# Hi and lo parts of the weights written from the second element of tiles one element longer

## The chip, the cores and the metric

The kernel runs on one NeuronCore of one Trainium2 chip. The metric is the device time of one execution, in microseconds. The engines named below are PE (TensorE, the matrix engine), PEld (its weight loads, which the profile lists by themselves), DVE (VectorE), ACT (ScalarE), POOL (GpSimd) and SP (SyncE, which only issues transfers here). Of the kernel before, three runs are known and one profiled execution.

## The reference

One step of a hybrid decoder layer in 32-bit floats, for 512 prompt tokens and 8 sample tokens, 520 columns together, with a model width of 2048:

```
xn   = rmsnorm(x) ; proj = xn @ w_in            # 2048 x 6160
ya   = bg * causal_conv3(cg * hin)              # short convolution, 1024 channels
yb   = rmsnorm(gla(q, k, v, gate)) * silu(og)   # gated linear attention, 4 heads
x    = x + concat(ya, yb) @ w_out               # 2048 x 2048
u, v = split(rmsnorm(x) @ w_up)                 # 2048 x 11264
x    = x + (silu(causal_conv3(u) + b) * v) @ w_down   # 5632 x 2048
y    = rmsnorm(x)
```

The outputs are y for both kinds of tokens and the new states of the convolutions and of the attention. Nearly all of the arithmetic is in the four products with `w_in`, `w_out`, `w_up` and `w_down`.

## The kernel before

Activations lie transposed: 128 channels on the partitions, 520 token columns along them, cut into two halves of 260 columns (`HT`). A matmul holds a 128 x 128 block of weights still and streams 260 columns past it.

Each operand is kept as two parts. The hi part is the value as the format `float32r` holds it (the ACT copy rounds it), the lo part is what is left. A product is then three matmuls, hi with hi, hi with lo and lo with hi (`mm3`, and the same three in `up_product` and `chunk_product`). For the weights this goes piece by piece: a piece of 128 x 1024 weights is loaded into a tile `raw`, ACT writes its hi part into a tile `hi`, DVE subtracts and writes the lo part into a tile `lo`, and PE reads eight 128 x 128 blocks from each. The pool `wp` keeps three tiles each of `raw`, `hi` and `lo`, of 1024 elements a partition.

There are two ways in which pieces are made:

- `parts` (lines 107 to 116) in the first stage, the plain products (`group`, with the matmuls on line 140), and again at the very end. ACT writes `hi` on line 111 and DVE writes `lo` on line 112.
- `prepare` (lines 1179 to 1200) in the long middle of the program. There the two-by-two blocks of a matrix product are multiplied in seven products instead of eight, some of them with sums of weight blocks (`raw`, or the sum tile `s`) as the source. ACT writes `hi` on line 1194, DVE writes `lo` on line 1198. Products are numbered by `order`; the loop calls `prepare(i + 2)` right after it has issued the matmuls of product `i`, so a piece is made about two products ahead of its use. `up_product` (matmuls on line 1218) and `chunk_product` (line 1461) use one hi and one lo tile for 24 matmuls.

The order of the work on PE, DVE and ACT, and in stretches on POOL and SP, is the program's own: `InOrder` ties each instruction to the one before it on its engine. Weights come over SP's queue; POOL's queue carries the stores of the activations' parts and some sums made by transfers that add. After the first stage follow a mixing stage with nine groups of seven products, eight groups for `w_out`, 44 for `w_up` and 20 for `w_down`, and then the end with plain products and the last norm.

For the steps of the prediction these places matter too: `conv_rest` (line 530) reads a padded tile from its second element (`i` is 1) and then from its first; `level` (lines 894 and 897) multiplies every other run of elements, and at the last of its seven levels, where a run is one element, line 894 reads and writes every second element beginning with the second, and line 897 every second beginning with the first. The matmul on line 943 holds 32 columns still instead of 128. At the end, one half of the tokens has 264 columns and the other 256.

Of the kernel before, what the change touches and what calls it, by code (L numbers as in the profile page):

```python
# [10 lines left out]
F32R = mybir.dt.float32r  # L11
# [6 lines left out]
P = 128  # L18
# [19 lines left out]
def trunk_kernel(  # L38
# [12 lines left out]
    wp = ctx.enter_context(tc.tile_pool(name="weights", bufs=3))  # L51
# [47 lines left out]
    def load(w, k0, nk, c0, ncol):  # L99
# [4 lines left out]
        )  # L104
        return raw, nk

    def parts(raw, nk):
        n = raw.shape[1]
        hi = wp.tile([P, 1024], F32R, tag="hi", name="hi")[:, :n]
        lo = wp.tile([P, 1024], F32R, tag="lo", name="lo")[:, :n]  # L110
        nc.scalar.activation(hi, raw, AF.Copy)  # L111
        nc.vector.tensor_tensor(lo, raw, hi.bitcast(F32), op=ALU.subtract)  # L112
        return (
            hi.rearrange("p (k c) -> p k c", k=nk),
            lo.rearrange("p (k c) -> p k c", k=nk),
        )

    def piece(*where):
        return parts(*load(*where))
# [157 lines left out]
    with ExitStack() as es:  # L277
# [164 lines left out]
        x_split(0)  # L442
        warm(8)
        ws = [parts(raws[0], 8)]
        x_copy(1)
        x_split(1)
# [4 lines left out]
        for k in range(KD):  # L451
# [11 lines left out]
            if t == 1 and c < 3:  # L463
                ws.append(parts(raws[c + 1], 8))
# [701 lines left out]
    state, his, los = {}, {}, {}  # L1166
# [12 lines left out]
    def prepare(i):  # L1179


        def sum_next():
            if i + 1 < len(order):
                kind, at, r = order[i + 1]
                if r in state[kind, at]["sums"]:
                    state[kind, at]["sums"][r]()

        if i >= len(order):
            return
        in_place = i + 1 < len(order) and order[i + 1][2] == 6  # L1190
        kind, at, r = order[i]
        src = state[kind, at]["src"][r]
        his[i] = wp.tile([P, 1024], F32R, tag="hi", name="hi")
        nc.scalar.activation(his[i], src, AF.Copy)  # L1194
        if not in_place:
            sum_next()
        los[i] = wp.tile([P, 1024], F32R, tag="lo", name="lo")
        nc.vector.tensor_tensor(los[i], src, his[i].bitcast(F32), op=ALU.subtract)  # L1198
        if in_place:
            sum_next()  # L1200
# [433 lines left out]
    ps = new_mm()  # L1634
    span(ps, ws[0], xa, 0, 0, 8, KD)
    prepare(0)
    for x in put[:3]:
        x()
    span(ps, ws[1], xa, 8, 8, 8, KD)
    prepare(1)  # L1640
    for x in put[3:6]:
        x()
# [25 lines left out]
    for i, (kind, at, r) in enumerate(order):  # L1668
        j, n = i % 7, i // 7
# [41 lines left out]
        if i in (0, 2, NW, NW + 2):  # L1711

            x = xq[1, 0][0]
            for ps in new[:2] if i in (0, NW) else new[2:]:
                nc.tensor.matmul(ps[:, :HT], x[:, :P], x, start=True, stop=True)
        prepare(i + 2)
        if j == 5 and more:
            state[groups[n + 1]]["seventh"]()
# [187 lines left out]
```

## Time and profile before

| | |
|---|---|
| runs | 2180.01, 2180.38, 2180.81 us |
| median of the runs | 2180.38 us |
| profiled execution, its span | 2180.4 us |
| instructions | 43803 |
| PE, busy | 2152.9 us, 99% |
| PEld, busy | 2131.3 us, 98% |
| DVE, busy | 1735.7 us, 80% |
| ACT, busy | 1114.0 us, 51% |
| POOL, busy | 438.1 us, 20% |

The profile is of one execution. Its span and the median of the runs are the same number to the tenth of a microsecond. A matmul's own duration in the records is longer than the distance from its start to the next one's start, since matmuls overlap in the pipeline; so the rate of PE is read from starts, or from the number of matmuls in a stretch. "hi" and "lo" in a row are the weights' parts; yh, yl, b, bh, bl, xh, xl, ch, cl and form are tiles of activations, which stream past.

### The profile page before, as it was taken

Reading aid. Unit: us, or ns where it says so; the run is one execution under the profiler, and the core shown is the slowest. Engines: PE = TensorE matmul, PEld = TensorE weight load, DVE = VectorE, ACT = ScalarE, POOL = GpSimd, SP = SyncE. Lnnn points to the kernel's source line nnn. Section 1 sums busy time; section 2 is a strip of 40 time slices with the busy share of each in tenths; the row PEclk is TensorE's granted clock in tenths of the full one; section 3 lists DMA queues with packets and bytes.
Section 4 is the critical chain, followed back from the end, with each engine's and each line's share of the span. In section 5 each row is a group of like instructions: output and inputs, shape, how many; then the busy total and the mean of one; then the engine's idle time right before and its main releaser. Section 6 shows DMA issues by size and latency. Waiting matters only on the chain.

```text
span 2180.4 us, 43803 instructions
## 1 busy us (share of the span) xinstructions
PE 2152.9 (99%) x17751; PEld 2131.3 (98%) x17751; DVE 1735.7 (80%) x2298; ACT 1114.0 (51%) x1625; POOL 438.1 (20%) x625
## 2 busy tenths in 40 slices
PE   9999999999999999999999999999999999999997
PEld 8999999999999999999999999999999999999997
DVE  6346465578888897988888988998998778888886
ACT  6335435355544586555555555555555553444445
POOL 4213131121243321121221131122111310010000
PEclk9999999999999999999999999999999999999999
DMA  8545464387788996667676676676677886894734
GB/s 247 147 125 158 122 191 124 92 246 210 204 257 248 297 266 176 179 178 187 164 189 174 165 195 176 163 194 177 171 186 190 285 202 197 248 271 132 226 107 156
DMA packets 467163, 415.51 MB, mean 191 GB/s; under 512 B 21641, under 2 KB 426393, under 8 KB 466817
## 3 DMA queue, kind: packets, MB, share of 16 engines
q1 hardware_dynamic: 424081, 289.71, 46.5%
q0 software_dynamic: 42832, 122.93, 21.4%
q8 instruction: 139, 2.28, 0.4%
q14 instruction: 63, 0.52, 0.1%
q10 hardware_dynamic: 48, 0.07, 0.0%
HBM read 299.45 MB, written 80.31 MB: 174 GB/s over the span
## 4 chain that ended last, share of the span: by engine, by line
PE 88%; DMA 4%; DVE 3%; issue 1%; ACT 1%; POOL 1%; SPq 0%; ACTq 0%; DVEq 0%; POOLq 0%
PE mm L1218 34%; PE mm L140 16%; PE ms L1218 14%; PE y L1461 7%; PE x L1461 7%; PE f L1461 3%; PE e L1461 3%; PE ms L957 1%; DMA raw<-in_w_out_dram 1%; DMA form<-g_d 1%; DVE lo L1198 1%; DMA g_d<-fh 1%; DMA x_d<-acc 1%; DMA yl<-t_d 0%; DMA raw<-in_w_down_dram 0%
## 5 line engine op out<-in xcount | busy, mean ns | idle before, releaser
L1218 PE MATMUL mm<-yl,hi 128*128 128x260 f32 x1696 | 479.8, 283 | 3.6 <-DVE yl L124 3.6
L1218 PE MATMUL mm<-yh,hi 128*128 128x260 f32 x1696 | 480.5, 283 | 2.1 <-ACT ms L1228 1.8
L1218 PE MATMUL mm<-yh,lo 128*128 128x260 f32 x1696 | 479.8, 283 | 0.8 <-DVE lo L1198 0.8
L1194 ACT ACTIVATE hi<-raw 128x1024 fp32r<-128x1024 f32 x324 | 342.6, 1057 | 233.9 <-PE mm L1218 69.0
L1198 DVE TENSOR_TENSOR lo<-raw,hi 128x1024 fp32r<-128x1024 f32 x324 | 395.2, 1220 | 41.2 <-ACT hi L1194 40.7
L1198 DVE TENSOR_TENSOR lo<-s,hi 128x1024 fp32r<-128x1024 f32 x243 | 298.3, 1228 | 127.2 <-ACT hi L1194 121.9
L1194 ACT ACTIVATE hi<-s 128x1024 fp32r<-128x1024 f32 x243 | 256.9, 1057 | 217.2 <-DVE s L1139 80.2
L1218 PEld LDWEIGHTS mm<-yl,hi 128*128 128x128 f32 x1696 | 320.1, 189 | 4.2 <-DVE yl L124 4.2
L1218 PEld LDWEIGHTS mm<-yh,hi 128*128 128x128 f32 x1696 | 319.7, 189 | 2.7 <-ACT ms L1228 2.0
L1218 PEld LDWEIGHTS mm<-yh,lo 128*128 128x128 f32 x1696 | 320.4, 189 | 1.2 <-DVE lo L1198 1.2
L1218 PE MATMUL ms<-b,hi 128*128 128x260 f32 x1408 | 257.8, 283 | 0.0
L1218 PEld LDWEIGHTS ms<-b,hi 128*128 128x128 f32 x1408 | 218.5, 190 | 0.0
L1461 PE MATMUL x<-form,hi 128*128 128x260 f32 x1120 | 204.6, 283 | 0.8 <-DVE acc L1480 0.8
L1461 PE MATMUL y<-form,hi 128*128 128x260 f32 x1120 | 204.5, 282 | 0.5 <-DVE acc L1480 0.5
L1139 DVE TENSOR_TENSOR s<-s,raw 128x1024 f32<-128x1024 f32 x162 | 197.8, 1221 | 2.8
L1218 PE MATMUL ms<-b,lo 128*128 128x260 f32 x704 | 199.5, 283 | 0.0
L1461 PEld LDWEIGHTS x<-form,hi 128*128 128x128 f32 x1120 | 172.4, 188 | 1.2 <-issue 1.0
L1461 PEld LDWEIGHTS y<-form,hi 128*128 128x128 f32 x1120 | 172.5, 188 | 0.8 <-issue 0.7
L1461 PE MATMUL y<-form,lo 128*128 128x260 f32 x560 | 158.2, 283 | 0.8 <-DVE lo L1198 0.8
L1461 PE MATMUL x<-form,lo 128*128 128x260 f32 x560 | 158.1, 282 | 0.0
L112 DVE TENSOR_TENSOR lo<-raw,hi 128x1024 fp32r<-128x1024 f32 x76 | 93.7, 1238 | 78.2 <-ACT hi L111 71.6
L1218 PEld LDWEIGHTS ms<-b,lo 128*128 128x128 f32 x704 | 133.4, 190 | 0.0
(366 smaller groups left out, 5077.8 us busy)
## 6 DMA issues: line engine op xcount, KB each, us to landing
raw<-in_w_up_dram SPq DMA_DIRECT2D x176, 512.0 KB, 4.7
raw<-in_w_down_dram SPq DMA_DIRECT2D x96, 512.0 KB, 5.5
raw<-in_w_in_dram SPq DMA_DIRECT2D x92, 512.0 KB, 4.4
form<-f_d SPq DMA_DIRECT2D x126, 260.0 KB, 6.8
raw<-raw POOLq DMA_DIRECT2D x56, 512.0 KB, 5.5
f_d<-t POOLq DMA_DIRECT2D x80, 260.0 KB, 5.5
raw<-in_w_out_dram SPq DMA_DIRECT2D x32, 512.0 KB, 12.7
form<-g_d POOLq DMA_DIRECT2D x42, 260.0 KB, 7.7
```

The lines of the kernel that those rows point to most:

```text
L112: nc.vector.tensor_tensor(lo, raw, hi.bitcast(F32), op=ALU.subtract)
L140: nc.tensor.matmul(o, w, xx, start=first and i == 0, stop=last and i == 2)
L957: nc.tensor.matmul(pb[:, c * 64 : (c + 1) * 64], L[:, c, :], rhs[:, c], start=True, stop=True,)
L1139: return lambda: nc.vector.tensor_tensor(out, x, y, op=ALU.add)
L1194: nc.scalar.activation(his[i], src, AF.Copy)
L1198: nc.vector.tensor_tensor(los[i], src, his[i].bitcast(F32), op=ALU.subtract)
L1218: nc.tensor.matmul(st["bank"][b], w[:, k, :], x, start=b not in st["used"] and k == 0 and j == 0, stop=k == 7 and j == 2, skip_group_check ...
L1461: nc.tensor.matmul(ps[:, m, :], w[:, k, m * P : (m + 1) * P], x, start=b not in st["used"] and k == 0 and j == 0, stop=k == 3 and j == 2, ...
```

## The change

The tiles of the weights' parts get 1025 elements a partition instead of 1024, and what is written and read is the slice from the second element on. Both places where such tiles are made now call the same small function; nothing else is changed. The elements written and read, the instructions, their order and their waits are the same as before. The first element of each tile is neither written nor read. The data of each part so begins 4 bytes behind the start of its tile, and the six tiles take a little more of each partition.

```diff
+    def offset(tag):
+
+        return wp.tile([P, 1025], F32R, tag=tag, name=tag)[:, 1:]
+
     def parts(raw, nk):
         n = raw.shape[1]
-        hi = wp.tile([P, 1024], F32R, tag="hi", name="hi")[:, :n]
-        lo = wp.tile([P, 1024], F32R, tag="lo", name="lo")[:, :n]
+        hi, lo = (offset(tag)[:, :n] for tag in ("hi", "lo"))
         nc.scalar.activation(hi, raw, AF.Copy)
         nc.vector.tensor_tensor(lo, raw, hi.bitcast(F32), op=ALU.subtract)
...
-        his[i] = wp.tile([P, 1024], F32R, tag="hi", name="hi")
+        his[i] = offset("hi")
         nc.scalar.activation(his[i], src, AF.Copy)
         if not in_place:
             sum_next()
-        los[i] = wp.tile([P, 1024], F32R, tag="lo", name="lo")
+        los[i] = offset("lo")
         nc.vector.tensor_tensor(los[i], src, his[i].bitcast(F32), op=ALU.subtract)
```

## The prediction

> **What bounds the kernel now.** I read the page's busy shares first, then its chain of work that ended last, then the table of windows.
>
> ```profile
> PE 2152.9 (99%) x17751; PEld 2131.3 (98%) x17751; DVE 1735.7 (80%) x2298; ACT 1114.0 (51%) x1625; POOL 438.1 (20%) x625
> ...
> PEclk9999999999999999999999999999999999999999
> ...
> PE 88%; DMA 4%; DVE 3%; issue 1%; ACT 1%; POOL 1%; SPq 0%; ACTq 0%; DVEq 0%; POOLq 0%
> ```
>
> PE is busy for 99% of the span at the full granted clock, and 88% of the chain is PE's. The span, 2180.4 us, and the median of the runs, 2180.38 us, agree, so I add and subtract from 2180.4 directly. The windows say how fast PE goes and what the others do meanwhile (columns: length, then busy time and instructions of PE, PEld, DVE, ACT and POOL, clock, DMA share, GB/s):
>
> ```profile
> 412.00:600.00 188.00, 185.20 (x1519) 184.17 (x1518) 149.25 (x204) 95.67 (x140) 37.35 (x53) 0.99 0.75 202
> 600.00:780.00 180.00, 179.50 (x1494) 179.09 (x1494) 154.13 (x176) 96.84 (x132) 68.26 (x94) 1.00 0.91 262
> ...
> 1200.00:1400.00 200.00, 200.00 (x1672) 200.00 (x1672) 177.91 (x239) 108.32 (x161) 41.55 (x60) 1.00 0.69 179
> ...
> 1900.00:2100.00 200.00, 200.00 (x1673) 200.00 (x1672) 167.76 (x170) 84.17 (x90) 9.20 (x12) 1.00 0.62 186
> ```
>
> In 1200 to 1400 us, 1672 matmuls start in 200 us, one each 119.6 ns. From 1900 to 2100 us DVE, ACT, POOL and the transfers do less, other tiles stream past, and the number is 1673. So the step of 119.6 ns does not depend on how busy the others are. It is PE's own, and the kernel's time is roughly that step times the matmuls. One nanosecond on each of the matmuls that use hi and lo is worth 17 us: they are 567 pieces of the middle part (324 and 243 in the rows of line 1198 below) times 24, 13,608, and those of the 76 pieces of line 112; 17,751 is the number of all matmuls. I use 17,000.
>
> **The change, part by part.** No instruction, byte of transfer or wait is added or removed. What moves is an address: three kinds of access now begin at an odd 4-byte word. These are ACT's writes of hi, DVE's reads of hi and writes of lo, and PE's loads from both.
>
> ```profile
> L1194 ACT ACTIVATE hi<-raw 128x1024 fp32r<-128x1024 f32 x324 | 342.6, 1057 | 233.9 <-PE mm L1218 69.0
> L1198 DVE TENSOR_TENSOR lo<-raw,hi 128x1024 fp32r<-128x1024 f32 x324 | 395.2, 1220 | 41.2 <-ACT hi L1194 40.7
> L1198 DVE TENSOR_TENSOR lo<-s,hi 128x1024 fp32r<-128x1024 f32 x243 | 298.3, 1228 | 127.2 <-ACT hi L1194 121.9
> ...
> L112 DVE TENSOR_TENSOR lo<-raw,hi 128x1024 fp32r<-128x1024 f32 x76 | 93.7, 1238 | 78.2 <-ACT hi L111 71.6
> ```
>
> DVE first. The trace has contiguous reads from an odd word: line 530 reads its padded tile from the second element, and two rows later from the first. It also has writes to odd words, though one element at a time: the last level on line 894, beside line 897 on even ones.
>
> ```profile
> 210.88 0.41 DVE L894 TENSOR_TENSOR L<-e,q 128x256 f32<-128x256 f32 x1
> 211.22 0.41 DVE L897 TENSOR_TENSOR L<-e,k 128x256 f32<-128x256 f32 x1
> ...
> 1006.91 0.74 DVE L530 SCALAR_TENSOR_TENSOR t<-zpad,parf,t 128x512 f32<-128x512 f32 x1
> 1007.58 0.22 DVE L533 SCALAR_TENSOR_TENSOR t<-stf,parf,t 128x8 f32<-128x8 f32 x1
> 1007.71 0.74 DVE L530 SCALAR_TENSOR_TENSOR t<-zpad,parf,t 128x512 f32<-128x512 f32 x1
> ```
>
> 0.74 against 0.74 us and 0.41 against 0.41 us: odd reads and odd writes cost nothing that shows. The lower end for a lo is therefore 0; for the upper end I take the dearest instruction of this kind beside a plain one of its length, both scalar_tensor_tensor with two tensors:
>
> ```profile
> L612 DVE SCALAR_TENSOR_TENSOR t<-t 128x260 f32<-128x260 f32 x56 | 23.8, 425 | 0.9
> ...
> L930 DVE SCALAR_TENSOR_TENSOR s<-s,asm,vb 128x256 f32<-128x256 f32 x32 | 20.5, 676 | 15.2 <-issue 5.2 <-ACT vb L927 4.8 <-DMA s<-in_state_gla_dram 3.8
> ```
>
> 676 / 425 = 1.6, or 0.73 us more on 1.22 us. I take 0, the value of the nearest rows. The cover is DVE's idle time: in 1200 to 1400 us it is 200 - 177.9 = 22.1 us, and about 70 pieces are made there (1672 / 24), so up to 22.1 / 70 = 0.32 us a piece costs nothing but slack.
>
> [...]
>
> ACT's write of hi has no odd row beside it. It is bounded by 0 and, by the same 1.6, 0.63 us on 1.06 us; ACT is busy 108.3 of 200 us there, so even 70 x 0.63 = 44 us fits. A piece is made two products ahead, 2 x 24 x 119.6 ns = 5.7 us before PE wants it, and hi and lo together could grow by 1.36 us inside that. If this cover failed, the next to be late would be PE, in the wait for lo that its rows show at 0.8 us or so now.
>
> PE's weight loads remain, and these nothing covers but PE's own step.
>
> ```profile
> L1218 PEld LDWEIGHTS mm<-yh,lo x1696: 186/188/334, 463.7 to 1707.2; 128*128 128x128 f32 x189
> ...
> L1461 PE MATMUL x<-form,lo x560: 277/282/296, 647.2 to 2098.1; 128*128 128x260 f32 x187
> L1461 PEld LDWEIGHTS y<-form,lo x560: 186/188/193, 650.2 to 2112.4; 128*128 128x128 f32 x187
> ```
>
> ```profile
> L943 PEld LDWEIGHTS ms<-s,qm x64: 106/108/110, 113.1 to 393.8; 128*32 128x32 f32 x64
> ```
>
> A load of 128 columns takes 188 ns, one of 32 columns 108 ns (min/median/max): (188 - 108) / 96 = 0.83 ns a column, so 107 ns of the 188 are the columns and the rest overlaps. 107 ns fit into a step of 119.6 ns with 13 ns to spare. That the streamed columns and not the load set the step is seen at the end of the program, where 264 and then 256 columns stream past the same kind of load:
>
> ```profile
> 2121.56 0.28 PE L140 MATMUL mm<-bh,lo 128*128 128x264 f32 x1
> ...
> 2122.66 0.28 PE L140 MATMUL mm<-bh,lo 128*128 128x264 f32 x1
> ```
>
> ```profile
> 2152.30 0.28 PE L140 MATMUL mm<-bl,hi 128*128 128x256 f32 x1
> ...
> 2153.36 0.28 PE L140 MATMUL mm<-bl,hi 128*128 128x256 f32 x1
> ```
>
> Nine steps lie between the two rows each time: 1.10 us / 9 = 122 ns and 1.06 / 9 = 118 ns. If an odd start adds one access to a load, a column's 0.83 ns or a few of them, it vanishes in the 13 ns.
>
> What the trace can't say is whether the load and the stream disturb each other. The durations of undisturbed matmuls spread from 277 over 282 to 296 ns in the row of line 1461 above, although columns and clock are the same. So something of PE's own varies by -5 to +14 ns, and I take these as the two ends for the unknown effect of the odd start on the step: -5 x 17,000 = -85 us and +14 x 17,000 = +238 us. I take 0, since no row ties the spread to the weights' first word. The sum is 2180.4 + 0 = 2180.4 us.
>
> **The rivals.**
> *Loads and streams collide less (faster).* For it: the step is 119.6 ns though the load needs 107, the matmuls vary among themselves, and the other engines' load does not explain it. Against it: nothing shows the start word as the cause. At half of the lower end, -2.5 ns, the time is 2180.4 - 42 = 2138 us; at the whole, 2095 us.
> *The load pays for the odd start (slower).* The place is the load of every 128 x 128 block, and it decides once the columns of a load need more than 119.6 instead of 107 ns, 12% more, or once they disturb the stream. At a quarter of the upper end, +3.5 ns, the time is 2180.4 + 60 = 2240 us; at the whole 2418 us. Against it: the 13 ns to spare.
> *DVE pays for the odd start (slower).* It decides from 0.32 us a piece. At the upper end, 0.73 us, DVE needs 177.9 + 70 x 0.73 = 229 us for each 200 us of the middle part, 15% more for the 900 us from 800 to 1700 us, and 167.8 + 51 = 219 us, a tenth more, for the 400 us behind them: 135 + 40 us, near 2355 us. The rows of lines 530 and 894 speak against it. [...]
> *Only the other tiles' moved places matter.* The six tiles grow, so all that lies behind them moves. A shift of 0.3 to 0.6 ns in the step, either way, is 5 to 10 us: 2170 or 2190 us.
>
> **How the numbers follow.** No change that can be measured: 0.42, with its own range of 2176 to 2185 us. Less collision: 0.28. The load pays: 0.16. DVE pays: 0.06. Moved places: 0.08, half each way. A measurement of this kernel tells 0.2%, 4.4 us, from no change. So faster is 0.28 + 0.04 = 0.32, the same 0.42, slower 0.16 + 0.06 + 0.04 = 0.26. The likeliest is 2180.4 us. The range has to reach into both sides: down to 2105 us, which leaves out the last part of the first rival (about 0.06), and up to 2240 us, which leaves out half of the load's rival and most of DVE's (about 0.13).
>
> **What would show it.** If I am right, 200 us of the middle part still hold 1672 matmuls, loads stay at 188 ns, lo at 1.22 us, hi at 1.06 us, and PE's idle time before lo stays near 1 us. More matmuls in 200 us, with DVE unchanged, would be the first rival; fewer, with PE still without idle time, the second; lo beyond 1.5 us and PE idle behind DVE's lo the third. The forecast is wrong if the count in such a window differs by more than 3 from 1672.

## The result and the profile after

The kernel with the longer tiles takes 2186.66 us (median, 2186.07 to 2189.67) against 2180.38 us (2179.46 to 2181.16). The ratio is 1.0032, with a 95% interval of 1.0021 to 1.0043: slower by 0.3%. That lies inside the range given, but further from the likeliest case, no change at all, than the 0.2% that the prediction took for measurable.

The page of the kernel after, its span and its busy times:

```profile
span 2188.0 us, 43803 instructions
...
PE 2160.2 (99%) x17751; PEld 2138.0 (98%) x17751; DVE 1737.7 (79%) x2298; ACT 1115.2 (51%) x1625; POOL 438.7 (20%) x625
```

PE has 7.3 us more busy time (2152.9 before), DVE 2.0 and ACT 1.2 us more; the span grew by 2188.0 - 2180.4 = 7.6 us. So PE's growth is nearly the whole of it. (These are two single executions, and that of the changed kernel was the longest of its seven runs; the medians lie 6.3 us apart.) The windows of the kernel after (columns as above):

```profile
600.00:780.00 180.00, 179.11 (x1485) 178.36 (x1484) 153.07 (x178) 95.36 (x131) 69.52 (x95) 1.00 0.89 260
...
1200.00:1400.00 200.00, 200.00 (x1665) 200.00 (x1664) 178.16 (x240) 108.32 (x161) 41.52 (x60) 1.00 0.67 176
...
1900.00:2100.00 200.00, 200.00 (x1667) 200.00 (x1666) 167.81 (x169) 83.29 (x90) 9.19 (x12) 1.00 0.61 186
```

PE still has no idle time in the middle part and the clock is full, but 200 us now hold 1665 matmuls and not 1672: by the count the step is 120.12 ns where it was 119.62. (A window also counts the two or three matmuls that begin before it and reach into it. Of the 1672, 1670 start in the window; steps taken from the starts, as below, are therefore 0.2 ns longer, for every kernel alike.) Near the end there are 1667 for 1673. What feeds PE is unchanged, as the groups of the kernel after show (line numbers are 3 higher):

```profile
L1201 DVE TENSOR_TENSOR lo<-raw,hi 128x1024 fp32r<-128x1024 f32 x324 | 396.2, 1223 | 44.0 <-ACT hi L1197 43.4
L1197 ACT ACTIVATE hi<-raw 128x1024 fp32r<-128x1024 f32 x324 | 343.2, 1059 | 236.8 <-PE mm L1221 69.0 <-issue 62.7 <-PE y L1464 25.7
...
L1221 PE MATMUL mm<-yh,lo 128*128 128x260 f32 x1696 | 480.7, 283 | 0.9 <-DVE lo L1201 0.9
```

A lo takes 1223 ns for 1220, a hi 1059 for 1057, and PE's idle time before lo is 0.9 us for 0.8. The loads keep their time too:

```profile
L1464 PEld LDWEIGHTS y<-form,lo x560: 187/188/194, 653.1 to 2119.8; 128*128 128x128 f32 x187
L1464 PE MATMUL y<-form,lo x560: 277/282/388, 653.2 to 2119.9; 128*128 128x260 f32 x187
```

188 ns, and 282 ns for a matmul, are the medians of before. The loss is therefore in no single instruction; it is in the distance between them. I took the distances from each matmul's start to the next one's, for the matmuls of the plain, mix, up, `w_out` and down products, wherever a distance lay between 100 and 140 ns in both traces (16,635 of them):

| kernel | all three | plain (L140) | mix and up (L1218) | w_out and down (L1461) | matmuls in 1200-1400 us |
|---|---|---|---|---|---|
| before | 119.86 ns | 120.08 | 119.80 | 119.81 | 1672 |
| after | 120.28 ns | 120.56 | 120.29 | 120.08 | 1665 |

16,635 x 0.425 ns = 7.1 us of the 7.6 us lie in these steps, spread over the whole program. The rest, 0.5 us, lies elsewhere.

Theory A: an odd word at the start of a block costs PE's step. Theory B: the odd word is innocent, and the growth of the tiles is at fault, since it puts each weights' tile at another distance from the last and moves the tiles behind it.

### The profile page after: what moved, and what is told of

Read it like the earlier page. It is cut to its first block, busy times and chain, and to the rows that moved or that the text cites. A ratio compares the mean times of both kernels' runs of the same rounds, so it can differ in the third digit from the quotient of the medians.

```text
span 2188.0 us, 43803 instructions
## 1 busy us (share of the span) xinstructions
PE 2160.2 (99%) x17751; PEld 2138.0 (98%) x17751; DVE 1737.7 (79%) x2298; ACT 1115.2 (51%) x1625; POOL 438.7 (20%) x625
## 4 chain that ended last, share of the span: by engine, by line
PE 60%; DMA 2%; DVE 1%; issue 1%; ACT 0%; POOL 0%; ACTq 0%; DVEq 0%; SPq 0%; POOLq 0%
PE mm L1221 29%; PE ms L1221 12%; PE y L1464 6%; PE x L1464 6%; PE f L1464 3%; PE e L1464 3%; PE mm L143 2%; DMA ssq<-fh 1%; DMA x_d<-acc 1%; DMA raw<-in_w_down_dram 0%; PE ms L1804 0%; DVE lo L1201 0%; DMA yl<-t_d 0%; DVE yl L127 0%; DVE s L1142 0%
## 5 line engine op out<-in xcount | busy, mean ns | idle before, releaser
L1197 ACT ACTIVATE hi<-raw 128x1024 fp32r<-128x1024 f32 x324 | 343.2, 1059 | 236.8 <-PE mm L1221 69.0
L1201 DVE TENSOR_TENSOR lo<-raw,hi 128x1024 fp32r<-128x1024 f32 x324 | 396.2, 1223 | 44.0 <-ACT hi L1197 43.4
L1197 ACT ACTIVATE hi<-s 128x1024 fp32r<-128x1024 f32 x243 | 257.4, 1059 | 217.5 <-PE ms L1221 86.2
```

## The experiments

All times in this table are medians of their own runs, the ratio is to runs of the kernel before beside them on the same chip, and the steps are worked out as above.

| run | us | ratio, 95% interval | step, ns | matmuls in 1200-1400 us |
|---|---|---|---|---|
| e1_grow | 2180.63 | 0.9999 (0.9990 to 1.0008) | 119.91 | 1670 |
| e2_ring0 | 2179.47 | 0.9997 (0.9988 to 1.0006) | 119.87 | 1672 |
| e3_ring1 | 2185.74 | 1.0024 (1.0014 to 1.0034) | 120.29 | 1663 |
| e4_off4 | 2181.33 | 1.0000 (0.9991 to 1.0009) | 119.89 | 1670 |
| e5_hi1 | 2188.92 | 1.0032 (1.0020 to 1.0043) | 120.34 | 1663 |
| e6_lo1 | 2184.68 | 1.0011 (1.0002 to 1.0020) | 120.04 | 1669 |
| e7_off2 | 2184.00 | 1.0011 (1.0002 to 1.0020) | 120.02 | 1670 |
| e11_slices3 | 2172.06 | 0.9964 (0.9951 to 0.9976) | 119.20 | 1679 |
| e12_slices0 | 2179.75 | 1.0001 (0.9992 to 1.0010) | 119.86 | 1673 |

### Growth without the offset

```diff
-        return wp.tile([P, 1025], F32R, tag=tag, name=tag)[:, 1:]
+        return wp.tile([P, 1025], F32R, tag=tag, name=tag)[:, :1024]
```

> The tiles of hi and lo are 1025 elements wide as in the changed kernel, but their first 1024 elements are used, so nothing begins at an odd word. Theory A (the odd 4-byte word costs the step of PE): back to 1671-1673 matmuls in 1200-1400 us and 2180 us. Theory B (the places count: each tile begins 4128 instead of 4096 bytes behind the one before, and the tiles behind them move by 96 to 192 bytes): as the changed kernel, about 1665 matmuls there and 2185-2188 us, and not the same in each of its places.

The windows of this run:

```profile
1200.00:1400.00 200.00, 200.00 (x1670) 200.00 (x1670) 177.90 (x238) 108.13 (x161) 41.06 (x60) 1.00 0.67 178
```

1670 matmuls and 2180.63 us: the growth and everything that it moves cost nothing that the times can tell. Theory B, as put, falls.

### The offset without the growth

In place of three tiles each, one tile holds three slices 4096 bytes apart. The two runs differ in one digit, the 1 ahead of the plus, which is 0 in the first of them:

```diff
+    rings = {t: [wp.tile([P, 3080], F32R, tag=t, name=t, bufs=1), 0] for t in ("hi", "lo")}
     def offset(tag):
-        return wp.tile([P, 1025], F32R, tag=tag, name=tag)[:, 1:]
+        rings[tag][1], d = rings[tag][1] + 1024, 1 + rings[tag][1] % 3072
+        return rings[tag][0][:, d : d + 1024]
```

> The three hi tiles are one tile with three slices 1024 elements (4096 bytes) apart, used in turn, and the same for lo; data from the first element. This is the kernel before with the tiles behind moved by 32 to 64 bytes. Theory A and theory B in its part on the distance of the tiles: as before, 1672 matmuls in 1200-1400 us, 2180 us. If only the places of the tiles behind count: another number, 2170-2190 us.

> As the kernel with the slices in one tile, 4096 bytes apart, but each from one element later: the odd word alone, with distance and size kept. Theory A: about 1665 matmuls in 1200-1400 us and 2187 us. Theory B: the same as the slices from the first element, within 2 matmuls and 3 us. Loads 188 ns, lo 1.22 to 1.23 us either way.

The windows of the run with slices from the first element, and then of the run with slices from the second:

```profile
1200.00:1400.00 200.00, 200.00 (x1672) 200.00 (x1672) 178.12 (x238) 108.01 (x161) 41.29 (x60) 1.00 0.66 179
...
1900.00:2100.00 200.00, 200.00 (x1671) 200.00 (x1671) 167.63 (x170) 83.69 (x90) 9.21 (x12) 1.00 0.60 184
```

```profile
1200.00:1400.00 200.00, 200.00 (x1663) 200.00 (x1662) 177.44 (x238) 108.37 (x160) 41.63 (x60) 1.00 0.67 178
...
1900.00:2100.00 200.00, 200.00 (x1672) 200.00 (x1671) 167.77 (x171) 83.21 (x89) 9.21 (x12) 1.00 0.61 185
```

One element moved, nothing else, and the middle part falls from 1672 to 1663: the loss of the change is made by the offset alone. But the second row doesn't fit a price per odd load: from 1900 to 2100 us the blocks are just as odd and nothing is lost (1672 against 1671; the steps of the products of `w_out` and `w_down` are 119.87 and 119.85 ns), while the changed kernel loses 6 matmuls there.

### Other offsets, and one part at a time

```diff
# e4_off4
+        return wp.tile([P, 1028], F32R, tag=tag, name=tag)[:, 4:]
# e7_off2
+        return wp.tile([P, 1026], F32R, tag=tag, name=tag)[:, 2:]
# e5_hi1; e6_lo1 has "lo"
+        d = tag == "hi"
+        return wp.tile([P, 1025], F32R, tag=tag, name=tag)[:, d : d + 1024]
```

> The tiles are 1028 elements wide, which leaves the same distance of 4128 bytes between tiles, and the data begin at the fifth element, 16 bytes on, on an even word. Theory A (an odd word is what costs): as the kernel with grown tiles and no offset. Theory B: near the changed kernel, 1663 to 1669 matmuls in 1200-1400 us and 2183-2190 us, as any place with this distance gives.

> All six tiles 1025 elements wide; only the hi parts begin at the second element, the lo parts at the first. PE loads blocks of hi in two of three matmuls. Theory A1 (each load of a block that begins at an odd word costs its step the same): two thirds of the 0.43 ns that the odd word cost, so about 1667 matmuls in 1200-1400 us and 2184.5 us. Theory A2 (DVE, which reads hi and writes lo, is what costs): no loss that PE's count shows.

> As the one before with only the lo parts from the second element. Theory A1: a third of the loss, about 1669 matmuls in 1200-1400 us and 2182.5 us.

> Tiles of 1026 elements, which leaves the tiles 4128 bytes apart, with the data from the third element, 8 bytes on. If what counts is the 8-byte boundary: as the grown tiles without offset, 1670 matmuls in 1200-1400 us and 2180.6 us. If it is a boundary of 16 bytes: as the changed kernel, 1663-1665 matmuls and 2186 us.

The windows of the run with only the hi parts offset:

```profile
1200.00:1400.00 200.00, 200.00 (x1663) 200.00 (x1662) 177.10 (x238) 108.25 (x160) 41.54 (x60) 1.00 0.68 177
...
1900.00:2100.00 200.00, 200.00 (x1665) 200.00 (x1664) 167.58 (x169) 83.22 (x89) 9.19 (x12) 1.00 0.61 186
```

16 bytes cost nothing (ratio 1.0000, step 119.89 ns), 8 bytes 0.1% (its interval just leaves out no change), so neither boundary of the expectation is clean. And the parts don't add up. The hi parts alone cost 16,632 x 0.483 = 8.0 us of steps, more than both together (7.1) where two thirds of it were expected, and the lo parts alone 3.1. With only hi offset the plain products lose nothing (120.12 ns against 120.08), with both they lose 0.48 ns. A fixed price for each odd load would add up and would show in every stage. It does neither.

ACT writes, and DVE reads and writes, at odd words too. Do they get in PE's way? In 1000 to 1600 us the steps that ACT fills (by over 90%) are 120.36 ns in the changed kernel and 119.98 with growth alone; those in which it rests (under 10%) are 120.28 and 119.85. With DVE filling the step it is 120.33 against 119.94, with DVE at rest 120.23 against 119.89 (some 425 steps each, about 0.2 ns of uncertainty). The loss is thus the same 0.3 to 0.4 ns whether they work or not, and so it is not tied to their work. Transfers were not told apart in this way.

### PE alone: is it the relation of two places?

What else can an offset do? It changes the relation of two places, and that this sets the step is called theory R below: where the block that is being loaded lies against the slice that streams past meanwhile. Two signs of this are in the traces of the whole kernel. First, in the kernel before, between 1000 and 1600 us, the steps of the 24 matmuls of a product come back every 7 products to 0.2 ns (mean deviation from the median), whatever the data; in the changed kernel every 21, to 0.3 ns, while at 7 they deviate by 1.5. 21 is 7 times the three weights' buffers. Second, the slices 4096 bytes apart return at 7 with the odd word as without it (0.2 and 0.3 ns), and the grown tiles without an offset, 4128 bytes apart, return at 21 only (0.3; 1.5 at 7). So the steps of one product are no noise, and they follow the places of the buffers. To see it without the other engines, PE got a kernel to itself:

```diff
+    def pair(o, d, m, first, last):
+        nc.tensor.matmul(o, w[:, d : d + P], x[:, m : m + HT], start=first, stop=last)
...
+    for d in (0, 1, 2, 3, 4, 8):
+        for i in range(1104):
+            pair(ps["o%d" % d], d + P * (i % 24), HT * (i * 5 % 23), i == 0, i == 1103)
```

> The model is left out: zeros are written to the outputs, and PE multiplies blocks of one tile of weights with slices of 260 columns of one tile, in order and without other engines. Tiles o0, o1, o2, o3, o4 and o8: 1104 matmuls each, blocks and slices in a fixed changing order, with every block 0, 1, 2, 3, 4 or 8 words further on. Then 20 matmuls each on one block and one slice, for many pairs of places. Theory A: the step of o0 is 119.9 ns, o4 and o8 the same within 0.2 ns, o1 and o3 0.4 to 0.5 ns more; o2 tells the boundary of 8 from that of 16 bytes. If the odd word costs only while other engines use the memory, all six are alike.

The windows of this run, one inside each of the six stretches (block further on by 0, 1, 2, 3, 4 and 8 words):

```profile
60.00:185.00 125.00, 125.00 (x1042) 125.00 (x1041) 0.00 (x0) 0.00 (x0) 0.00 (x0) 1.00 0.00 1
195.00:320.00 125.00, 125.00 (x1047) 125.00 (x1046) 0.00 (x0) 0.00 (x0) 0.00 (x0) 1.00 0.00 1
325.00:450.00 125.00, 125.00 (x1047) 125.00 (x1046) 0.00 (x0) 0.00 (x0) 0.00 (x0) 1.00 0.00 1
460.00:585.00 125.00, 125.00 (x1043) 125.00 (x1043) 0.00 (x0) 0.00 (x0) 0.00 (x0) 1.00 0.00 1
590.00:715.00 125.00, 125.00 (x1040) 125.00 (x1039) 0.00 (x0) 0.00 (x0) 0.00 (x0) 1.00 0.00 1
725.00:850.00 125.00, 125.00 (x1046) 125.00 (x1045) 0.00 (x0) 0.00 (x0) 0.00 (x0) 1.00 0.00 1
```

From the first to the last start of each stretch of 1104, the steps are 120.28, 119.72, 119.71, 120.01, 120.57 and 119.71 ns. With PE alone the step is thus as long as in the full kernel, and here one word further is not dearer but cheaper (119.72), four words dearer (120.57). The order of the even ones among themselves, 120.28, 119.71, 120.57 and 119.71 ns at 0, 2, 4 and 8 words, spreads as widely as the whole effect asked about. The other part of the run, whose loop is not shown, holds one slice still and moves one repeated block by 8 words at a time. Eight steps (the mean from the third start of 20 to the last) return in every 64 words, sixteen times over, within 0.24 ns:

```
block moved by, words (mod 64)     0      8     16     24     32     40     48     56
mean step, ns                  118.6  120.1  119.9  120.0  121.3  120.6  120.0  120.4
```

The stream is the same in all eight. So, for one pair that repeats, the place of the load changes the step, by up to 2.7 ns (118.6 to 121.3), with a period of 64 words, 256 bytes.

The scan took all places of the block and eight of the slice:

```diff
+    for m in range(8):
+        for d in range(64):
+            for i in range(20):
+                pair(ps["one"], d, m, i == 0, i == 19)
```

> The model is left out as in the run of pairs before; PE works alone. Tile one: 20 matmuls each on one block and one slice, the block 0 to 63 words from the start of the weights' tile, the slice 0 to 7 words from the start of its own. Tile two: the same with two slices 260 columns apart taken in turn. Theory R (what counts is where the block lies against the slice, and it repeats every 64 words): the step depends on the difference of the two places and on the slice's place modulo 8 words, between 117 and 124 ns, and in each row odd and even words of the block come out alike on the mean within 0.3 ns. Theory A (an odd word of the block costs by itself): in each row the odd words are 0.4 ns or more above the even ones.

The windows of this run, 145 us inside the stretches with the slice from word 0, 1, 2 and 3:

```profile
60.00:205.00 145.00, 145.00 (x1210) 145.00 (x1209) 0.00 (x0) 0.00 (x0) 0.00 (x0) 1.00 0.00 1
215.00:360.00 145.00, 145.00 (x1182) 145.00 (x1181) 0.00 (x0) 0.00 (x0) 0.00 (x0) 1.00 0.00 1
372.00:517.00 145.00, 145.00 (x1198) 145.00 (x1197) 0.00 (x0) 0.00 (x0) 0.00 (x0) 1.00 0.00 1
525.00:670.00 145.00, 145.00 (x1223) 145.00 (x1222) 0.00 (x0) 0.00 (x0) 0.00 (x0) 1.00 0.00 1
```

The count falls and rises with the slice's word, from 1210 to 1182, 1198 and 1223. Mean step over the 64 places of the block, and over the even and the odd ones of them, worked out from the starts:

```
slice from word     0       1       2       3       4       5       6       7
all            119.98  122.86  121.45  118.78  119.89  123.06  121.53  119.24
even blocks    120.04  122.75  121.40  118.94  120.00  123.18  121.35  119.20
odd blocks     119.92  122.97  121.51  118.62  119.78  122.94  121.70  119.28
```

Even and odd blocks differ by 0.35 ns at most, in either direction; over the eight rows the odd ones lie 0.02 ns lower, with 0.12 of uncertainty, so a price of 0.4 ns falls for a repeated pair. With two slices in turn (tile two) the odd blocks lie 0.48 ns higher for the slices from word 0, with 0.27 of uncertainty, and alike for those from word 4. Theory R is borne out in part: the steps of the pairs (mean of 20) reach from 117.4 to 126.8 ns, beyond its 124, and moving block and slice by 4 words together does not bring a step back (the correlation over the 64 places is -0.1 to 0.3). So both places count, but not by their difference alone; whether the difference counts at one place of the slice modulo 8 words, the scan's eight slices cannot tell. Something else stands out, which I had not looked for: the slice's own start modulo 4 words moves the step by 4 ns.

A pair that repeats may fall into a rhythm that a changing sequence has not, so the last run on PE alone draws its places:

```diff
+    for t, o in ps.items():
+        m, d = ("zbcd".index(x.replace("a", "z")) for x in t)
+        for i in range(n):
+            pair(o, 4 * (places[i] % 1000) + d, 4 * places[n + i] + m, i == 0, i == n - 1)
```

> The model is left out as in the runs of pairs and the scan; PE works alone, 1600 matmuls each into eight tiles, always with the same drawn order of places, all multiples of 4 words, to which a remainder is added. za, zb, zc, zd: slice at remainder 0, block at 0, 1, 2, 3. bz, cz, dz: slice at 1, 2, 3, block at 0. db: slice at 3, block at 1. Theory A (the odd word of a block costs PE by itself): za and zc near 119.9 ns a step, zb and zd 0.4 ns or more above them. Theory R (only the relation of the two places counts, and the changed kernel drew a dear one): za, zb, zc and zd alike within 0.15 ns. On the slice, by the scan: dz and db near 119.0 ns, cz 121.5, bz 123; if the scan's rows hold only for one pair repeated, these are near 120 too.

PE's matmuls into each of the tiles (number, duration min/median/max, first and last start; za has 200 more at its start, which are left out below):

```profile
L77 PE MATMUL za<-x,w x1800: 277/282/556, 20.9 to 238.4; 128*128 128x260 f32 x180
...
L77 PE MATMUL zb<-x,w x1600: 277/282/297, 238.5 to 430.4; 128*128 128x260 f32 x178
...
L77 PE MATMUL zc<-x,w x1600: 277/282/295, 430.6 to 622.2; 128*128 128x260 f32 x178
...
L77 PE MATMUL zd<-x,w x1600: 277/282/297, 622.4 to 814.3; 128*128 128x260 f32 x178
...
L77 PE MATMUL bz<-x,w x1600: 278/286/298, 814.4 to 1010.6; 128*128 128x260 f32 x178
...
L77 PE MATMUL cz<-x,w x1600: 278/284/309, 1010.7 to 1205.8; 128*128 128x260 f32 x178
...
L77 PE MATMUL dz<-x,w x1600: 277/280/291, 1205.9 to 1396.0; 128*128 128x260 f32 x178
...
L77 PE MATMUL db<-x,w x1600: 277/280/291, 1396.1 to 1586.4; 128*128 128x260 f32 x178
```

The stretch between the two starts over 1599 steps gives 122.7 ns for bz, 122.0 for cz, 118.9 for dz and 119.0 for db, much as the scan's rows had it. From the single starts, za is 119.97, zb 120.05, zc 119.87 and zd 120.03, alike within 0.18 ns where theory R had 0.15, each to 0.07 ns (2.7 ns of spread over the root of 1600). Odd blocks are dearer by (120.05 + 120.03 - 119.97 - 119.87) / 2 = 0.12 ns, with the same 0.07 of uncertainty. That is a quarter of the 0.43 to 0.48 ns that the three kernels with odd hi parts lose, and hardly more than nothing. (From dz to db it is 0.17 ns, on one pair of tiles.) Nor does theory R hold here for single steps: in none of the eight tiles does the distance of the block from the slice, modulo 64 words, together with the slice's place modulo 8, account for more than 4% of their variance, for the matmul's own block or the next one (2% are chance). What one pair gave when it repeated did not carry over to the single steps of this drawn order.

### A version that beats both: the slices moved instead

If a slice that begins 3 words behind a multiple of 4 words makes the step 1.1 ns shorter, as the drawn places say, the streamed tiles should be moved and not the weights. In the kernel before, every such slice begins at a multiple of 4 words. The tiles of activations were joined to rows, to have room for the three words; `act` stands for their allocation:

```diff
+    def act(pool, dtype, tag, name):
+        if tag[0] == "x" or pool is slots[0]:
+            d = START if pool is slots[0] or tag[:2] in PADDED else 0
+            return pool.tile([P, T + d], dtype, tag=tag, name=name)[:, d:]
...
+            row = pool.tile([P, n * T + START], F32R, name=name)
...
+        return row[:, START + i * T : START + (i + 1) * T]
```

`START` is 3 in the first run and 0 in the second.

> The whole model, with the weights' tiles of the kernel before. The tiles of activations that stream past are placed so that 15,256 of the matmuls' slices begin 3 words behind a multiple of 4 words; they are rows of one larger tile where that was needed for room (the names in the trace are then the row's), and 1,764 slices stay at a multiple of 4. By the run of drawn places a step is 119.97 - 118.86 = 1.11 ns shorter there: 15,256 x 1.11 = 17 us, so about 2163 us, and 1686 to 1688 matmuls in 1200-1400 us. If DVE, ACT or the transfers pay for the odd places of the activations, less, and PE shows idle time behind them.

> The same placing in larger tiles with every slice at a multiple of 4 words. If the 3 words are what counts: 2176 to 2185 us, 1667 to 1676 matmuls in 1200-1400 us, no more than another draw of places. If the joined tiles are what counts: as the run with 3 words.

The windows of the run with 3 words, and then of the run with 0:

```profile
1200.00:1400.00 200.00, 200.00 (x1679) 200.00 (x1679) 178.73 (x240) 108.87 (x161) 41.55 (x60) 1.00 0.68 179
...
1900.00:2100.00 200.00, 200.00 (x1683) 200.00 (x1682) 168.11 (x170) 85.42 (x91) 8.00 (x11) 1.00 0.59 181
```

```profile
1200.00:1400.00 200.00, 200.00 (x1673) 200.00 (x1672) 177.95 (x240) 109.42 (x161) 41.06 (x60) 1.00 0.67 177
```

2172.06 us, 0.36% faster than the kernel before; with 0 words in the same rows 2179.75 us, no change. So the gain comes from the three words. It is smaller than expected: the steps are 119.20 ns and not 119.86, 10.8 us over 16,624 of them, where I had put 17. Part of that is known: the kernel before drew a slightly better 119.86 than the 119.97 of drawn places, 0.11 ns x 15,256 = 1.7 us. In `w_out` and `w_down`, where every slice was moved, the step fell by 0.84 ns to 118.97, near the 118.86 of drawn places; in the mix and up products, where some slices stayed, by 0.52. The slices that stayed explain little of it, for the steps between two moved slices are 119.20 ns there; what keeps them behind was not tried.

The run with 0 words shows something more. In it every block of hi and lo, and every slice that streams past one, lies at the very address of the kernel before, although the tiles are joined, and so it is no other draw of places. Its single steps repeat those of the kernel before: in the mix and up products they differ by 0.37 ns on the mean, those of every other layout by 2.8 to 3.2 ns. Here, then, the same places in the same order gave the same steps, to 0.37 ns, and each changed layout drew all of them anew.

## Why the prediction was right or wrong, point by point

- **What bounds the kernel: right.** PE has no idle time in the middle part, and its time is the step times the matmuls. 7.1 of the 7.6 us between the profiled executions are steps.
- **DVE at +0: right.** A lo took 1223 ns for 1220 and ACT's hi 1059 for 1057, so that the cover was not needed. In that lo, hi and the output, but not raw, began at an odd word.
- **The load's own time, hidden in 13 ns to spare: right as far as it goes.** 188 ns before and after.
- **The unknown effect of load and stream on each other, taken at 0: this is the step that failed.** The prediction gave it -5 to +14 ns and wrote "I take 0, since no row ties the spread to the weights' first word". It is +0.43 ns over all steps (+0.50 in the middle part), which times 17,000 is the 7 us that were missing. The range of 135 us would have held every layout tried here, so that it held 2186.66 us says little. The sign was that of the rival "the load pays", through the words "or once they disturb the stream"; its size was an eighth of the 3.5 ns that the rival was priced with. The two ends were taken from the spread of single durations, 277 to 296 ns; the mean over 17,000 steps with many different places moved far less: the layouts tried here lie between 119.20 and 120.34 ns.
- **"Only the other tiles' moved places matter": its size of 0.3 to 0.6 ns and its 2190 us were near, its cause was wrong.** The same growth without the offset gave 119.91 ns and 2180.63 us.
- **Less collision (2138 us): not here.** A shorter step by another place does exist, on the other operand, and at 0.36%; that it comes from fewer collisions is not shown.
- **"The forecast is wrong if the count differs by more than 3 from 1672": it differs by 7.** By its own sign the forecast of no change is wrong, though the time lies in the range.

What is shown: the offset and not the growth costs the time, on PE's steps, whether DVE and ACT work or rest; and the steps follow the places of blocks and slices in their order. By which relation of the places, and why the odd word comes out dearer, stays open. All three layouts with odd hi parts lost 0.43 to 0.48 ns, while the five layouts with all weights at even words and all slices at multiples of 4 words lay at 119.86 to 120.02, so chance alone is a poor account (two of the three share their tiles' distances, though). Yet drawn places give 0.12 ns, the down products of one layout lose nothing, and the parts don't add up, so a price per odd word is a poor account too. The step of a given sequence could not be worked out from the scan either. Its values, taken at each matmul's slice modulo 8 words and the distance of the block from it, give 119.86 ns for before, but 120.01 for after where 120.28 was measured, and 120.12 for the offset of 16 bytes where 119.89 was.

## What to carry to other kernels

Where PE runs without a gap, its step is not only the number of columns (118.86 to 122.70 ns for the same 260 columns here): look at the count of matmuls in a window of the trace before and after any change that moves a tile, even one that adds no work. A change of address is not a change of nothing; forecast it as a small shift of either sign on the mean step (119.20 to 120.34 ns here, for 119.86 before), and not as zero. To see whether two layouts differ for PE at all, compare their single steps (0.37 ns apart here for the same places, 2.8 to 3.2 ns for others) and not only the mean. And try the streamed operand's start: here 3 words behind a multiple of 4 was the best of four places (118.86 ns for 119.97) and cost three words of room a row.

## What the runs showed of the hardware that was not expected

With blocks at multiples of 4 words and drawn places, PE's step for 260 columns of 4-byte words was 119.97 ns for slices that begin at a multiple of 4 words, and 122.70, 122.01 and 118.86 ns for 1, 2 and 3 words behind it.

For one slice and one repeated block, the step repeats when the block moves by 256 bytes, and varies by 2.7 ns in between (118.6 to 121.3). In the whole kernel, too, the steps return when the buffers' places do: after 7 products with buffers 4096 bytes apart (to 0.2 and 0.3 ns), after 21 with 4128 (to 0.3 ns).
